# Conditioning rows on GpSimd's queue, eight weight sums shifted, the first head's weights written ahead of its tables, one Silu a gate chunk

## The chip, the cores and the metric

One core of one Trainium2 chip runs the kernel. The metric is device time of one execution in microseconds; three runs of the kernel before took 1923.67, 1926.17 and 1926.65 us, so the median is 1926.17 us. A further execution was taken with the hardware profiler, and all rows of a profile come from it. Its own time is 1929.21 us, and 1927.4 us of that are the span between its first and its last recorded instruction.

TensorE is called PE in the profile (PEld are its weight loads), VectorE is DVE, ScalarE is ACT, GpSimd is POOL and SyncE is SP. SP issues most of the loads from memory; ACT and POOL issue some transfers of their own.

## The reference

Two layers over 256 latent and 256 context tokens of width 2048. In each layer the tokens are normalised and modulated by a shift and a scale that come from a conditioning vector, then mixed, multiplied by a Silu gate, projected back, and added under a third conditioning vector, the output gate. Layer 0 mixes by retention in two directions (8 heads, keys of 256, values of 512), layer 1 by windowed attention (16 query heads, 4 key heads).

```
mod_l = silu(c) @ ada_w[i] + ada_b[i]         # shift, scale, gate of the latent tokens
mod_c = silu(c_ctx) @ ada_w[i] + ada_b[i]     # the same for the context tokens
h_l = rms_norm(x, g[i]) * (1 + sc_l) + sh_l
h_c = rms_norm(ctx, g[i]) * (1 + sc_c) + sh_c
layer 0: p = h @ ret_w_in                     # q, k, v, gate; 2048 x 12288
         o_c, s_f, s_b = retention(q_c, k_c, v_c)     # both directions
         o_l = retention(q_l, k_l, v_l, from s_f, s_b)
         y = (rms_norm(o) * silu(gate)) @ ret_w_out   # latent and context tokens
layer 1: o = attention(q, k, v within 128 tokens, all context keys, a sink)
         y = (o * silu(gate)) @ attn_w_out            # latent tokens alone
x = x + gt * y
```

Everything is fp32.

## The kernel before, in words

**Arithmetic.** Each fp32 operand of a matrix product is split into a high and a low part of a shorter type, and each product is three matmuls (`mm3`, L152 to L154: high by high, high by low, low by high). A weight arrives as a "piece" of 128 x 1024 numbers (512 KB): `load_raw` (L133 to L136) issues its load on SP into one of five buffers `wraw`; `split_w` makes the high part `wh` by a cast on ACT (L144) and the low part `wl` by a subtraction on DVE (L115), three buffers each. So a piece goes SP, DMA, ACT, DVE, PE.

**Stages**, with the times at which they run in the trace: the conditioning of layer 0 and the normalised tokens (to about 140 us), queries and keys of two heads (to about 240), the values (to about 548), the heads' gates, queries, keys and retention (to about 1165), the output projections of layer 0 (to about 1500), keys and values of layer 1, then its gates, queries and attention (about 1610 to 1845) and its output projection.

**The values** are computed for two heads at a time, four pairs, by a scheme that saves multiplications (Winograd's): weight pieces are added and subtracted on DVE into `vt` (L118), and these sums are split and multiplied. `VORDER` sets the order of the steps of a pair: four quarters, of 8, 8, 8 and 4 products X, Y, Z, each followed by `wide_hook`. A name such as "0X1" is quarter 0, product X, piece 1. Twelve matmuls make a step. Two tables say at which steps the hook also does other work: `WIDE_ADA` a step of the conditioning, `WIDE_SUMS` a weight sum.

**The conditioning of later parts** (`ada_parts`, L677 to L700) runs beside the values and the heads: pieces of `ada_w` are loaded by SP into the same `wraw` buffers, and DVE multiplies each by a conditioning row and adds up along it (L692). A row is 4 KB in memory, spread over all 128 partitions as it is loaded (`crow`, L672 to L675, 512 KB written); there is one for the latent and one for the context tokens, for each half of the width.

**Weight sums** (`sum_jobs`, L324 to L340) prepare weights for the output projections: a 256 KB half piece of the output weight is copied to memory by a transfer that ACT issues (L332), and three sums later POOL issues a transfer that adds a second half piece on top (L338). Ahead of each of these POOL makes a small copy (`pin`, L336) out of the newest `wl`, which keeps the transfer at its place. There are 128 sums. 14 are made beside each pair of values, others beside the heads, and what is left in the output projections' own stages.

**The heads** call `hook` (L1149) once per weight piece: up to hook 32 every second one makes a sum, from there on two of three (hooks count on to 88). The first head's gate is `gemm_ws(w0_d, 2, ...)`; ahead of it the program loads a table for the rotary embedding (`ropeR`, L953, L954) and the stored queries and keys (`qkr`, L1124).

**Layer 1's gates**: `gate(c)` (L1525 to L1531) makes four accumulators of 128 x 512; for each it copies the context half to `sgT` on ACT, adds the latent half on DVE, and applies Silu on ACT to a 128 x 256 tile. Between chunks ACT also computes the softmax's exponentials (L1563), which need another function table; ACT_TABLE_LOAD rows are the changes of table.

What the program's text says is not the final order: a scheduler puts each engine's instructions into a sequence by their dependences. The orders shown below are those sequences.

Of the kernel before, what the change touches and what calls it, by code (L numbers as in the profile page):

```python
# [14 lines left out]
AF = mybir.ActivationFunctionType  # L15
# [14 lines left out]
PUMP = 2  # L30
VORDER = ("X0 Z0 X1 Z1 X2 Z2 X3 Z3", "Y0 Z0 Y1 Z1 Y2 Z2 Z3 Y3", "X0 Y0 X1 Y1 X2 Y2 X3 Y3", "Y0 Y1 Y2 Y3")
WIDE_ADA = "3Y0 3Y1 3Y2 1Z0 1Z1 1Z2".split()
WIDE_SUMS = "0X1 0X3 1Y0 1Y1 1Z1 1Y2 1Z3 1Y3 2Y1 2Y2 2Y3 3Y1 3Y2 3Y3".split()
ASCALE = 128.0 ** -0.5


# [17 lines left out]
def backbone(ctx: ExitStack, tc, xT_d, w0_d, wo0_d, w1_d, wo1_d, adaS_d, adaB_d,  # L54
# [78 lines left out]
    def load_raw(src):  # L133
        t = strm.tile([P, 2, 512], F32, name="wraw", tag="wraw", bufs=5)
        nc.sync.dma_start(out=t, in_=src)
        return t  # L136

    def load_w(src):
        return split_w(load_raw(src))
# [13 lines left out]
        nc.tensor.matmul(ps, lhsT=ah, rhs=bl, start=False, stop=False, skip_group_check=skip)  # L153
        return nc.tensor.matmul(ps, lhsT=al, rhs=bh, start=False, stop=stop, skip_group_check=skip).ins  # L154

    def gemm_ws(w_d, chunk, nkp, moving, n, hook=None, pre=None, tail=1):


        accs = [acc_tile()[:, :n] for _ in range(4)]
        w = {}  # L160
        for kp in range(nkp):
            if pre is not None:
                pre(kp)
            w[kp] = load_w(w_d[chunk, kp])
            if kp < nkp - tail:
                kps = [kp]
            elif kp < nkp - 1:
                if hook is not None:
                    hook()
                continue  # L170
            else:
                kps = range(nkp - tail, nkp)
            for j in range(4):
                for kb in [2 * k + k2 for k in kps for k2 in range(2)]:
                    wh, wl = w[kb // 2]
                    js = slice(j * P, (j + 1) * P)
                    mm3(accs[j], (wh[:, kb % 2, js], wl[:, kb % 2, js]), moving(kb),
                        start=(kb == 0), stop=(kb == 2 * nkp - 1))
            if hook is not None:
                hook()  # L180
        return accs
# [215 lines left out]
    with tc.tile_pool(name="pa", bufs=1) as pa:  # L397
# [25 lines left out]
        def keep_warm(src, n=512):  # L423

            with after():
                pe[0] = nc.tensor.matmul(warm[:, :n], lhsT=ident, rhs=src[:, :n], start=True, stop=True).ins
# [146 lines left out]
        keep_warm(x01[:, 0, :])  # L573

        def first():
            keep_warm(x01[:, 1, :])
            strip(0, [2, 3])
            return pe[0]

# [87 lines left out]
    pb_cm.__exit__(None, None, None)  # L667


    rows_at = {}  # L670

    def crow(pool, tag, t, q, queue=nc.sync):  # L672
        c = pool.tile([P, 1024], F32, name="crow", tag=tag)
# [3 lines left out]
    def ada_parts(parts, ntk):  # L677
        for layer, kind in parts:
            part = 3 * layer + kind - 2
            asum = const.tile([P, 2, KB, ntk], F32, name="asum", tag=f"asum{ntk}")  # L680
            for q in range(2):
                if q not in rows_at:
                    rows_at.clear()
                    rows_at[q] = [crow(adap[0], f"crow{t}", t, q) for t in range(ntk)]
                    yield "row"
                for kb in range(KB):
                    raw = load_raw(adaB_d[16 * part + kb, q].rearrange("p (a c) -> p a c", a=2))
                    yield "load"
                    for t in range(ntk):
                        flat = raw.rearrange("p a c -> p (a c)")  # L690
                        junk = adap[0].tile([P, 1024], BF16, name="ajunk", tag="ajunk") if t < ntk - 1 else flat
                        nc.vector.scalar_tensor_tensor(  # L692
                            out=junk, in0=flat, scalar=1.0, in1=rows_at[q][t],
                            op0=ALU.mult, op1=ALU.mult, accum_out=asum[:, q, kb, t:t + 1])
                        if (kb, t) != (KB - 1, ntk - 1):
                            yield
                if q:
                    sh, gs, gt = (sh0, gs0, gt0) if layer == 0 else (sh1, gs1, gt1)
                    nc.vector.tensor_tensor(out=asum[:, 0], in0=asum[:, 0], in1=asum[:, 1], op=ALU.add)
                    ada_mod(kind, layer, 0, KB, asum[:, 0], sh, gs, gt, ntk)  # L700
                yield "end"
# [241 lines left out]
    def prep(m, us):  # L943
# [3 lines left out]
        for i, u in enumerate(us):  # L947
            b = unit(m, u)
            with behind():
                split(b[:, :, 0:L], b[:, :, L:T], raw[:, i])  # L950

    if True:
        ropeR = pb.tile([P, 2, 68], F32, name="ropeR")  # L953
        nc.sync.dma_start(out=ropeR, in_=ropeR_d)  # L954
# [193 lines left out]

        def hook():  # L1149
            state["n"] += 1  # L1150
            if state["n"] % 2 == 0 if state["n"] <= 32 else state["n"] % 3 < 2:
                next(sums, None)
            ada_step(next(state["ada"]))
            for x in next(state["plan"]):
                x()
# [12 lines left out]
        for h in range(H):  # L1168
# [12 lines left out]
            else:  # L1181
# [4 lines left out]
                if h == H - 1:  # L1186
                    break
                begin([[], [], [], [sc[0]], [sc[1]], [sc[2]], [sc[3]], []], (1, 3, 3, 2, 2, 2, 2, 3))
            accs = gemm_ws(w0_d, 3 * h + 2, 8, h_mov, T, hook=hook)
            sg = gates(h)  # L1190
            for j in range(4):
                nc.scalar.activation(sg[j // 2][:, j % 2, :], accs[j], AF.Silu)
# [273 lines left out]
    with tc.tile_pool(name="pe", bufs=1, side="right") as pe:  # L1466
# [58 lines left out]
        def gate(c):  # L1525
            accs = gemm_ws2(w1_d, 2 + c, 8, 0, hook=hook1)
            for j in range(4):
                z = sgT[:, 4 * c + j, :]
                nc.scalar.copy(z, accs[j][:, L:T])
                nc.vector.tensor_tensor(out=z, in0=accs[j][:, 0:L], in1=z, op=ALU.add)  # L1530
                nc.scalar.activation(z, z, AF.Silu)  # L1531

        def queries(c):
            accs = gemm_ts(w1_d, 6 + c, 8, h1_stat, 2, hook=hook1)
# [212 lines left out]
```

## Time and profile before

| what | value |
| --- | --- |
| runs | 1923.67, 1926.17, 1926.65 us; median 1926.17 us |
| profiled execution | 1929.21 us, its span 1927.4 us |
| PE busy | 1906.4 us, 99% of the span |
| PE's weight loads | 1577.9 us, 82% |
| DVE busy | 1477.2 us, 77% |
| ACT busy | 822.0 us, 43% |
| POOL busy | 324.5 us, 17% |
| mean granted clock of PE | 0.998 |
| bytes moved by DMA | 472.82 MB, mean 245 GB/s |

PE's row in the page's picture of 40 slices shows 8 tenths in the first slice and 9 or more in every other. The chain of waits, which follows the end of the span back to what released it, is 89% PE, 5% DMA and 3% DVE.

How to read the rows: a timeline row has the start in us, the duration, the engine, the line of the program, the operation, and out<-in with the shape; the square bracket holds the idle time before and what ended it. A window row has the stretch, its length, busy time and instruction count of each engine, then PE's granted clock (1.00 is full speed), the mean busy share of the 16 DMA engines, and GB/s. A row of the waits has total, count and longest in us. A row of the DMA issues has the KB of one and its us from issue to landing.

### The profile page before, as it was taken

What the parts mean: (1) busy time and instruction counts of PE and PEld (TensorE: products, weight loads), DVE (VectorE), ACT (ScalarE), POOL (GpSimd) and SP (SyncE); (2) the same over time, 40 slices, a digit from 0 to 9 for tenths busy, and PEclk for the clock granted to TensorE, in tenths of its full rate; (3) what the DMA queues carried; (4) which work ended last, traced back from release to release, by engine and by line L of the source; (5) the groups of instructions that cost most, each with busy time, mean ns of one, the idle gap of its engine ahead of it and who ended that gap; (6) DMA issues with size and microseconds to landing.
All of it is one profiled execution on the core that took longest, in us unless ns stands there. A gap on an engine that the chain in (4) does not pass through costs nothing.

```text
span 1927.4 us, 25993 instructions
## 1 busy us (share of the span) xinstructions
PE 1906.4 (99%) x9420; PEld 1577.9 (82%) x9420; DVE 1477.2 (77%) x2248; ACT 822.0 (43%) x1188; POOL 324.5 (17%) x418
## 2 busy tenths in 40 slices
PE   8999999999999999999999999999999999999999
PEld 4678887888878888888888888888888888888888
DVE  5568876877858888797978676877779668988764
ACT  4232333443434333232323244555545335666653
POOL 1201112222222233323232211000000100000000
PEclk9999999999999999999999999999999999999999
DMA  9968788899897777888888765789975356665454
GB/s 391 415 260 281 254 241 268 262 275 292 248 276 246 238 237 220 252 261 252 269 248 264 241 214 196 244 274 301 305 256 199 115 175 240 216 220 177 140 202 150
DMA packets 139217, 472.82 MB, mean 245 GB/s; under 512 B 17696, under 2 KB 32576, under 8 KB 133456
## 3 DMA queue, kind: packets, MB, share of 16 engines
q1 hardware_dynamic: 107104, 368.31, 54.2%
q0 software_dynamic: 15424, 49.33, 13.2%
q10 hardware_dynamic: 16560, 53.51, 8.0%
q8 instruction: 74, 1.21, 0.2%
q14 instruction: 55, 0.45, 0.1%
HBM read 440.09 MB, written 99.14 MB: 280 GB/s over the span
## 4 chain that ended last, share of the span: by engine, by line
PE 89%; DMA 5%; DVE 3%; issue 1%; ACT 1%; SPq 0%; DVEq 0%; ACTq 0%
PE acc L153 15%; PE acc L154 15%; PE acc L152 15%; PE acc L1253 9%; PE acc L205 6%; PE acc L1250 5%; PE pm L152 4%; PE pm L153 4%; PE pm L154 4%; DMA wraw<-in_w 3%; PE acc L202 3%; PE acc L534 2%; PE pm L1253 2%; DVE wl L115 1%; PE pm L471 1%; DMA araw<-in_adaS 1%
## 5 line engine op out<-in xcount | busy, mean ns | idle before, releaser
L144 ACT CAST wh<-wraw 128x1024 fp32r<-128x1024 f32 x415 | 434.8, 1052 | 678.0 <-DMA wraw<-in_w 185.4
L115 DVE TENSOR_TENSOR wl<-wraw,wh 128x1024 fp32r<-128x1024 f32 x416 | 509.8, 1229 | 234.8 <-ACT wh L144 230.8
L152 PE MATMUL acc<-hT_h,wh 128*128 128x512 f32 x928 | 363.7, 392 | 1.0 <-ACT wh L144 1.0
L154 PE MATMUL acc<-hT_h,wl 128*128 128x512 f32 x928 | 362.2, 390 | 0.6 <-DVE wl L115 0.6
L153 PE MATMUL acc<-hl,wh 128*128 128x512 f32 x928 | 361.9, 390 | 0.0
L336 POOL COPY pin_t<-wl 128x1 f32<-128x1 f32 x128 | 78.2, 611 | 758.0 <-DVE wl L115 748.1
L154 PEld LDWEIGHTS acc<-hT_h,wl 128*128 128x128 f32 x928 | 174.5, 188 | 38.1 <-DVE wl L115 1.3
L152 PEld LDWEIGHTS acc<-hT_h,wh 128*128 128x128 f32 x928 | 174.8, 188 | 37.6 <-ACT wh L144 1.5
L153 PEld LDWEIGHTS acc<-hl,wh 128*128 128x128 f32 x928 | 174.8, 188 | 34.9
L692 DVE SCALAR_TENSOR_TENSOR wraw<-wraw,crow 128x1024 f32<-128x1024 f32 x128 | 159.4, 1245 | 0.3
L692 DVE SCALAR_TENSOR_TENSOR ajunk<-wraw,crow 128x1024 bf16<-128x1024 f32 x96 | 124.5, 1297 | 4.1 <-DMA wraw<-in_adaB 3.9
L154 PE MATMUL acc<-wh,hl 128*128 128x512 f32 x320 | 125.7, 393 | 0.0
L338 POOL DMA_DIRECT2D wS_d<-in_wo x128 | 101.5, 794 | 20.8 <-issue 18.6
L255 POOL TENSOR_TENSOR rs<-ms,mhalf 128x4 f32<-128x4 f32 (+1 forms) x23 | 30.7, 1333 | 386.4 <-DVE ms L249 297.4
L144 ACT CAST wh<-vt 128x1024 fp32r<-128x1024 f32 x48 | 50.6, 1053 | 79.0 <-PE acc L154 30.5
L153 PE MATMUL acc<-wl,hT_h 128*128 128x512 f32 x192 | 76.6, 399 | 4.6 <-DVE wl L115 4.5
L152 PE MATMUL acc<-wh,hT_h 128*128 128x512 f32 x192 | 75.5, 393 | 0.6 <-ACT wh L144 0.6
L153 PE MATMUL acc<-wl,hl 128*128 128x512 f32 x192 | 75.1, 391 | 0.0
L152 PE MATMUL acc<-wh,hl 128*128 128x512 f32 x192 | 75.0, 391 | 0.0
L152 PE MATMUL pm<-r_h 128*128 128x512 f32 (+1 forms) x216 | 74.5, 345 | 0.0
L153 PE MATMUL pm<-r_l,r_h 128*128 128x512 f32 (+1 forms) x216 | 74.2, 343 | 0.1
L154 PE MATMUL pm<-r_h,r_l 128*128 128x512 f32 (+1 forms) x216 | 73.9, 342 | 0.0
(324 smaller groups left out, 3612.4 us busy)
## 6 DMA issues: line engine op xcount, KB each, us to landing
wraw<-in_w SPq DMA_DIRECT2D x288, 512.0 KB, 5.1
wraw<-in_adaB SPq DMA_DIRECT2D x128, 512.0 KB, 4.8
wraw<-in_wo SPq DMA_DIRECT2D x80, 512.0 KB, 4.5
wS_d<-in_wo ACTq DMA_DIRECT2D x128, 256.0 KB, 4.9
wS_d<-in_wo POOLq DMA_DIRECT2D x128, 256.0 KB, 6.5
wraw<-wS_d SPq DMA_DIRECT2D x64, 512.0 KB, 5.3
araw<-in_adaS SPq DMA_DIRECT2D x28, 1024.0 KB, 13.1
wraw<-uB_d SPq DMA_DIRECT2D x20, 512.0 KB, 4.7
```

What stands on the lines that cost most here:

```text
L115: return nc.vector.tensor_tensor(out=out, in0=a, in1=hi.bitcast(F32), op=ALU.subtract)
L144: last_hi[0] = nc.scalar.copy(wh, raw).ins
L152: nc.tensor.matmul(ps, lhsT=ah, rhs=bh, start=start, stop=False, skip_group_check=skip)
L153: nc.tensor.matmul(ps, lhsT=ah, rhs=bl, start=False, stop=False, skip_group_check=skip)
L154: return nc.tensor.matmul(ps, lhsT=al, rhs=bh, start=False, stop=stop, skip_group_check=skip).ins
L202: nc.tensor.matmul(accs[j][:, 0:L], lhsT=wk, rhs=h1(kb, s)[:, 0], start=False, stop=(kb == 2 * nkp - 1))
L205: nc.tensor.matmul(accs[j], lhsT=wk, rhs=h1(kb, s).rearrange("p a t -> p (a t)"), start=(kb == 0), stop=False)
L336: pin = nc.gpsimd.tensor_copy(pin_t, last_wl[0][:, 0, 0:1].bitcast(F32)).ins
L338: nc.gpsimd.dma_start(out=wS_d[i, r, q, x], in_=wo0_d[(*SUMS[i][1], r, q, x)], accum_op=ALU.add, max_dma_last_dim=4096)
L692: nc.vector.scalar_tensor_tensor(out=junk, in0=flat, scalar=1.0, in1=rows_at[q][t], op0=ALU.mult, op1=ALU.mult, accum_out=asum[:, q, kb, t ...
L1250: last_pe[0] = nc.tensor.matmul(accs[j][:, 0:L], lhsT=wk, rhs=b[:, 0:L], start=False, stop=(kq == 3 and k == 3)).ins
L1253: nc.tensor.matmul(accs[j], lhsT=wk, rhs=b, start=(kq == 0 and k == 0), stop=False)
```

## The change

Five edits:

1. `WIDE_SUMS` loses "0X1" and "0X3", so each pair of values makes 12 sums instead of 14. In the heads, from hook 33 on, four of five hooks make a sum instead of two of three. 117 sums instead of 118 are issued by the end of the heads.
2. The first three gate pieces of the first head are loaded by a line ahead of the table `ropeR`, and `gemm_ws` takes them over (`raws`).
3. The first two conditioning rows that `ada_parts` loads stay on SP; all later ones are issued by GpSimd.
4. One of the matmuls that only warm PE at the start is gone (`keep_warm(x01[:, 1, :])`).
5. `gate(c)` applies one Silu to the 128 x 1024 of a chunk instead of four to 128 x 256 each.

```
-WIDE_SUMS = "0X1 0X3 1Y0 1Y1 1Z1 1Y2 1Z3 1Y3 2Y1 2Y2 2Y3 3Y1 3Y2 3Y3".split()
+WIDE_SUMS = "1Y0 1Y1 1Z1 1Y2 1Z3 1Y3 2Y1 2Y2 2Y3 3Y1 3Y2 3Y3".split()
...
-    def gemm_ws(w_d, chunk, nkp, moving, n, hook=None, pre=None, tail=1):
+    def gemm_ws(w_d, chunk, nkp, moving, n, hook=None, pre=None, tail=1, raws=()):
...
-            w[kp] = load_w(w_d[chunk, kp])
+            w[kp] = split_w(raws[kp]) if kp < len(raws) else load_w(w_d[chunk, kp])
...
         def first():
-            keep_warm(x01[:, 1, :])
             strip(0, [2, 3])
...
-    rows_at = {}
+    rows_at, queue = {}, [nc.sync]
...
-                    rows_at[q] = [crow(adap[0], f"crow{t}", t, q) for t in range(ntk)]
+                    rows_at[q] = [crow(adap[0], f"crow{t}", t, q, queue[0]) for t in range(ntk)]
+                    queue[0] = nc.gpsimd
...
+    early = [load_raw(w0_d[2, kp]) for kp in range(3)]
     if True:
         ropeR = pb.tile([P, 2, 68], F32, name="ropeR")
...
-            if state["n"] % 2 == 0 if state["n"] <= 32 else state["n"] % 3 < 2:
+            if state["n"] % 2 == 0 if state["n"] <= 32 else state["n"] % 5 < 4:
...
-            accs = gemm_ws(w0_d, 3 * h + 2, 8, h_mov, T, hook=hook)
+            accs = gemm_ws(w0_d, 3 * h + 2, 8, h_mov, T, hook=hook, raws=early if h == 0 else ())
...
-                nc.scalar.activation(z, z, AF.Silu)
+            z = sgT[:, 4 * c:4 * c + 4, :]
+            nc.scalar.activation(z, z, AF.Silu)
```

**The order on SP and POOL at the start of the second pair of values.** `wraw<-in_w0` are weight pieces of layer 0, `wraw<-in_adaB` pieces of the conditioning's weight, `crow<-crow_d` conditioning rows. SP before:

```order
L135 DMA wraw_2487<-in_adaB 128x1024
L135 DMA wraw_2492<-in_w0 128x1024
L135 DMA wraw_2515<-in_w0 128x1024
L135 DMA wraw_2540<-in_w0 128x1024
L674 DMA crow_2785<-crow_d_108 128x1024
L135 DMA wraw_2561<-in_w0 128x1024
L135 DMA wraw_2583<-in_w0 128x1024
L135 DMA wraw_2604<-in_w0 128x1024
```

SP now:

```order
L135 DMA wraw_2480<-in_adaB 128x1024
L135 DMA wraw_2485<-in_w0 128x1024
L135 DMA wraw_2508<-in_w0 128x1024
L135 DMA wraw_2533<-in_w0 128x1024
L135 DMA wraw_2554<-in_w0 128x1024
L135 DMA wraw_2576<-in_w0 128x1024
L135 DMA wraw_2594<-in_w0 128x1024
```

POOL now, where each `pin_t` and `wS_d` belong to a weight sum:

```order
L336 COPY pin_t_98<-wl_2488 128x1
L338 DMA wS_d_101<-in_wo0 64x1024
L673 DMA crow_2772<-crow_d_108 128x1024
L336 COPY pin_t_98<-wl_2513 128x1
L338 DMA wS_d_101<-in_wo0 64x1024
L336 COPY pin_t_98<-wl_2695 128x1
L338 DMA wS_d_101<-in_wo0 64x1024
L673 DMA crow_2774<-crow_d_108 128x1024
```

The row is gone from SP and stands on POOL between two sums; the second one, for the context tokens, follows it there two sums later. In all, four rows leave SP: these two, and two of layer 1's conditioning.

**SP where the heads begin.** `wraw<-in_w0` are now the first head's gate pieces, `wraw<-v_d` stored values, `ropeR` the table, `qkr` the stored queries and keys. Before:

```order
L135 DMA wraw_4325<-in_w0 128x1024
L135 DMA wraw_4355<-in_w0 128x1024
L135 DMA wraw_4388<-in_w0 128x1024
L135 DMA wraw_4429<-in_w0 128x1024
L135 DMA wraw_4475<-v_d_103 128x1024
L135 DMA wraw_4477<-v_d_103 128x1024
L954 DMA ropeR_4310<-in_ropeR 128x136
L1124 DMA qkr_4317<-qk_d_104 128x2x512
L1124 DMA qkr_4319<-qk_d_104 128x2x512
L135 DMA wraw_4479<-in_w0 128x1024
```

Now:

```order
L135 DMA wraw_4285<-in_w0 128x1024
L135 DMA wraw_4287<-in_w0 128x1024
L135 DMA wraw_4289<-in_w0 128x1024
L135 DMA wraw_4404<-in_w0 128x1024
L135 DMA wraw_4450<-v_d_103 128x1024
L135 DMA wraw_4452<-v_d_103 128x1024
L955 DMA ropeR_4291<-in_ropeR 128x136
L1125 DMA qkr_4298<-qk_d_104 128x2x512
L1125 DMA qkr_4300<-qk_d_104 128x2x512
L135 DMA wraw_4454<-in_w0 128x1024
```

The kinds of loads stand in the same sequence; the first three pieces have other buffer numbers.

**ACT at the third gate chunk of layer 1.** `sgT` is the gate, `prob` the softmax, `r2z_h` the high part of something that PE transposes next. Before:

```order
L1529 COPY sgT<-acc 128x256 x2
L1531 ACT_TABLE_LOAD
L1531 ACTIVATE sgT<-sgT 128x256
L1563 ACT_TABLE_LOAD
L1563 ACTIVATE prob,sm<-pm,nm 128x512
L1570 ACTIVATE es<-es 128x4
L1531 ACT_TABLE_LOAD
L1531 ACTIVATE sgT<-sgT 128x256
L1578 ACTIVATE prob<-prob,es 128x512 x2
L1529 COPY sgT<-acc 128x256 x2
L121 CAST r2z_h<-pm 128x512 x2
L1531 ACTIVATE sgT<-sgT 128x256 x2
```

Now:

```order
L1530 COPY sgT<-acc 128x256 x2
L1565 ACTIVATE prob,sm<-pm,nm 128x512
L1572 ACTIVATE es<-es 128x4
L1530 COPY sgT<-acc 128x256 x2
L144 CAST wh<-wraw 128x1024
L1580 ACTIVATE prob<-prob,es 128x512 x2
L1533 ACT_TABLE_LOAD
L1533 ACTIVATE sgT<-sgT 128x1024
L121 CAST r2z_h<-pm 128x512 x3
```

Two changes of table are gone; the Silu stands behind the softmax and directly ahead of the casts.

## The prediction

> **What bounds the kernel now.** I read the page's head first, then its chain of waits, then the table of 50 us windows, and only then the narrow windows, timelines and waits of the places that the diff touches.
>
> ```profile
> span 1927.4 us, 25993 instructions
> ...
> PE 1906.4 (99%) x9420; PEld 1577.9 (82%) x9420; DVE 1477.2 (77%) x2248; ACT 822.0 (43%) x1188; POOL 324.5 (17%) x418
> ...
> PE 89%; DMA 5%; DVE 3%; issue 1%; ACT 1%; SPq 0%; DVEq 0%; ACTq 0%
> ```
>
> PE is busy for 1906.4 of 1927.4 us. The change takes no matmul of weight away, so it can win only out of the 21.0 us in which PE stands idle, and out of matmuls that run slowly because the granted clock falls after a stall. The windows (us, then PE busy with its matmuls, PEld, DVE, ACT, POOL, granted clock, DMA share, GB/s) say where that lies.
>
> ```profile
> 0.00:50.00 50.00, 40.62 (x226) 21.36 (x230) 26.56 (x66) 20.39 (x30) 5.97 (x11) 1.00 0.98 392
> ...
> 300.00:350.00 50.00, 46.08 (x195) 37.30 (x194) 34.83 (x36) 18.02 (x19) 8.94 (x17) 0.97 0.86 259
> ...
> 550.00:600.00 50.00, 48.39 (x211) 39.45 (x210) 30.51 (x48) 16.87 (x23) 7.51 (x14) 0.97 0.85 270
> ...
> 1750.00:1800.00 50.00, 49.14 (x248) 40.69 (x247) 40.35 (x77) 36.78 (x62) 1.18 (x2) 1.00 0.50 171
> ```
>
> Idle of PE: 9.4 us in the first 50, 3.9 around the start of the second pair of value heads, 1.6 where the heads begin, 0.9 at layer 1's gates. These four are the places of the diff. Only 300 to 350 and 550 to 600 also show a clock under 1.00.
>
> **Edit A: the conditioning rows leave SP.** The second pair starts near 310. The same columns, in 4 us windows:
>
> ```profile
> 316.00:320.00 4.00, 4.00 (x19) 3.30 (x19) 0.72 (x1) 0.00 (x0) 0.96 (x2) 1.00 1.04 390
> 320.00:324.00 4.00, 2.39 (x10) 1.42 (x8) 0.10 (x1) 1.04 (x1) 0.00 (x0) 1.00 0.96 319
> 324.00:328.00 4.00, 1.69 (x6) 1.38 (x7) 3.95 (x4) 2.00 (x2) 0.00 (x0) 0.89 0.60 221
> 328.00:332.00 4.00, 4.00 (x14) 3.18 (x13) 3.09 (x4) 1.05 (x1) 0.00 (x0) 0.68 0.77 246
> 332.00:336.00 4.00, 4.00 (x20) 3.30 (x19) 2.48 (x3) 1.64 (x2) 0.96 (x2) 1.00 0.71 217
> ```
>
> The first and last rows give 39 matmuls in 8 us, 0.205 us each. The 12 us between hold 10 + 6 + 14 = 30 matmuls where 12 / 0.205 = 58.5 would fit: 28.5 x 0.205 = 5.85 us are lost, of which 3.9 are idle and 1.9 come from the clock of 0.89 and 0.68. What ends the longer wait, and what fed it (timeline of PE and DVE, then SP's queue; the bracket is the idle time before and its releaser):
>
> ```profile
> 326.31 0.51 PE L153 MATMUL acc<-wl,hT_h 128*128 128x512 f32 x1 [3.33 <-DVE wl L115]
> ...
> 323.89 1.22 DVE L118 TENSOR_TENSOR vt<-wraw 128x1024 f32<-128x1024 f32 x1 [7.18 <-DMA wraw<-in_w]
> ...
> 302.30 0.33 SPq L135 DMA_DIRECT2D wraw<-in_w  x1
> 306.43 0.33 SPq L674 DMA_DIRECT2D crow<-crow_d  x1
> 307.57 1.46 SPq L135 DMA_DIRECT2D wraw<-in_w  x2
> ```
>
> PE waits for a split, the split for VectorE's sum of two weight pieces, and that for a weight load 7.18 us. The late loads stand on SP just behind the conditioning row. Their landing times (narrow views of the DMA issues: KB each, us from issue to landing), the crow's, those of the two loads behind it, and of loads in the third pair's start, where no row is loaded:
>
> ```profile
> crow<-crow_d SPq DMA_DIRECT2D x1, 512.0 KB, 11.6
> wraw<-in_w SPq DMA_DIRECT2D x1, 512.0 KB, 13.7
> wraw<-in_w SPq DMA_DIRECT2D x1, 512.0 KB, 15.1
> ...
> wraw<-in_w SPq DMA_DIRECT2D x2, 512.0 KB, 11.2
> ```
>
> So the row landed at 306.43 + 11.6 = 318.0, 3.8 us behind the load ahead of it (302.30, landed at about 314.2), and the two loads behind it at 321.3 and 323.8. Without the row in that line they come up to 3.8 us earlier, at 317.5 and 320.0, and the 3.33 us wait at 323 to 326 has its cause gone. SP's own wait for the row's buffer frees nothing, since the next load would have waited as long:
>
> ```profile
> SPq L674 <- DVE ajunk L692: 3.7, 1, 3.7
> ```
>
> What is late next: starts of pairs that have no row in the way still lose a little (PE's columns only).
>
> ```profile
> 404.00:408.00 4.00, 3.32 (x15) 1.00 0.78 224
> 480.00:484.00 4.00, 3.74 (x17) 1.00 0.94 282
> ```
>
> They lose (19.5 - 15) x 0.205 = 0.9 and (19.5 - 17) x 0.205 = 0.5 us. I expect the second pair to look like them: 5.85 less about 0.45 leaves **5.4 us**; the bounds are 0 (the row only moves to another queue of the same DMA engines) and 5.85. The row itself is not urgent, on whichever queue; VectorE first multiplies by it here:
>
> ```profile
> 383.69 1.21 DVE L692 SCALAR_TENSOR_TENSOR ajunk<-wraw,crow 128x1024 bf16<-128x1024 f32 x1
> ```
>
> GpSimd issues it between two weight sums. Behind it wait only pin copies and accumulations, whose results nobody reads before the output projections.
>
> The Trainium skill bears on this from both sides. "DMA: Bandwidth & Descriptors", section "Issuing engines are not separate DMA queues", says that transfers of all engines run on the same 16 DMA engines and that another issuer mostly saves issue time: by it, A would be worth 0.33 us, the row's issue on SP. The section "Queues, rings and completion order" of the same page says that a DMA engine takes turns between the queues it has work for, one packet each: by it, a load behind the row no longer waits for the whole row, but shares with it. The trace shows a DMA share of 0.96 to 1.04 before and in the stall, which speaks for the first, and only 0.60 to 0.77 behind it.
>
> **Edit B: no weight sums at X1 and X3 of a pair's first quarter.** Two sums less in each pair's first 8 steps, eight in all. In the second pair their two transfers each (an ACT-issued copy and a GpSimd-issued accumulation) fall into the stall of A already counted; in the third and fourth they lie around the 0.9 and 0.5 us above. I take **1.0 us** of these 1.4 (bounds 0 and 1.4).
>
> Seven of the eight go to the heads, where four hooks of five now issue a sum, and one into the output projections. The queues of the accumulations and of the copies took this share of 16 engines' span:
>
> ```profile
> q0 software_dynamic: 15424, 49.33, 13.2%
> ...
> q10 hardware_dynamic: 16560, 53.51, 8.0%
> ```
>
> At most 21.2% of 1927 us for 128 sums is 3.2 us a sum; seven more, over 330 us of heads, are 0.07 of DMA share on top of this:
>
> ```profile
> 800.00:1130.00 330.00, 330.00 (x1530) 275.57 (x1529) 263.79 (x447) 103.20 (x163) 93.30 (x111) 1.00 0.82 252
> ```
>
> PE does not idle there for a moment. The smallest margin that I found between a weight's split and the matmul that uses it:
>
> ```profile
> 1025.30 1.22 DVE L115 TENSOR_TENSOR wl<-wraw,wh 128x1024 fp32r<-128x1024 f32 x1
> ...
> 1029.12 0.39 PE L154 MATMUL acc<-hT_h,wl 128*128 128x512 f32 x1
> ```
>
> It is 1029.12 - 1026.52 = 2.6 us, more than a load lengthens by if a share of 0.82 becomes 0.89. So **0**; the bound on the loss is a rival below.
>
> **Edit C: the first head's gate pieces ahead of its tables.** The stall where the heads begin (PE's columns, then SP's issues):
>
> ```profile
> 570.00:575.00 5.00, 3.39 (x9) 0.79 0.94 288
> 575.00:580.00 5.00, 5.00 (x21) 0.87 0.91 292
> ...
> 559.34 0.33 SPq L954 DMA_DIRECT2D ropeR<-in_ropeR  x1
> 561.08 1.06 SPq L135 DMA_DIRECT2D wraw<-in_w  x2
> ```
>
> 30 matmuls where 10 / 0.205 = 48.8 fit: 3.85 us lost, fed by the two pieces issued at 561.08 behind table and value loads. But the order of SP, shown above, has four gate pieces ahead of the table before the change already, and the same sequence after it: four pieces, two value loads, the table, two q/k loads, then the next pieces. Nothing moves, so **0**, with 3.85 as the upper bound.
>
> **Edit D: one Silu a gate chunk.** ScalarE's groups (busy and mean ns), then the one stall at these gates:
>
> ```profile
> L1531 ACT ACT_TABLE_LOAD x5 | 6.4, 1283 | 0.1
> L1531 ACT ACTIVATE sgT<-sgT 128x256 f32<-128x256 f32 x16 | 6.3, 422 | 0.1
> ...
> 1764.00:1768.00 4.00, 3.14 (x21) 1.00 0.00 0
> ...
> 1767.95 0.66 PE L1583 MATMUL pm<-ident,prob 128*128 128x128 f32 x4 [0.86 <-DVE r2z_l L115]
> ```
>
> Sixteen activations of 0.42 us become four longer ones, and two table loads of 1.28 us go. ScalarE has room almost everywhere (36.8 of 50 us busy in this very window), so only the 0.86 us count. At the third gate chunk the table loads that stood ahead of the softmax are gone, but the whole Silu now stands ahead of the casts r2z_h, which feed that same wait through VectorE: at worst a load and the work of four pieces, 1.28 + 4 x 0.42 = 3.0 us, is put in front. The matmuls that wait are also placed earlier in PE's order. I take **0.4 us** (bounds -3.0 and 0.86).
>
> **Edit E: one warming matmul less at the start.** In the first 50 us the DMA share is 0.98: PE waits for weights, not for its own work. A warming matmul takes half of this row:
>
> ```profile
> 18.96 1.10 PE L426 MATMUL pm<-x,ident 128*128 128x512 f32 x2
> ```
>
> So **0**, with its own 0.55 us as the bound on either side: gained, or lost again if the clock is granted that much later.
>
> **The sum.** 5.4 + 1.0 + 0 + 0.4 + 0 = 6.8 us. The profiled execution took 1929.21 us (1.8 more than its span); less 6.8 this is 1922.4, with a span of 1920.6. It was 3.0 us above the median of the runs, 1926.17, so the median should come out at 1926.17 - 6.8 = 1919.4. What a measurement of this kernel can tell from no change is about 0.2%, 3.85 us: faster means under 1922.3, slower over 1930.0.
>
> **The rivals.**
>
> *The row's bytes compete all the same (0.20).* The DMA engines are full until 324 in any queue, the two loads behind the row land as late as now, and A is worth nothing. For it: the share of 0.96 to 1.04. Against it: the row holds back its successors by 3.8 us on their own queue, and two sums leave the same stretch. B and D remain: 1926.17 - 1.4 = 1924.8, no change that can be told.
>
> *The early pieces do take effect (0.06).* If the first pieces are issued sooner in time, though not in another order, the 3.85 us of C come on top: 1919.4 - 3.85 = 1915.6. Against it: the unchanged order.
>
> *The heads pay for the sums (0.08).* With four hooks in five a GpSimd accumulation and a copy stand beside nearly each weight load of the later heads. If a load comes more than the 2.6 us of margin late, PE stalls and its clock falls as it does at 570, 3.85 us each time; once in each of heads 4 to 7 it is 15.4 - 6.8 = 8.6 us more than now, 1934.8. It decides from a loss of 6.8 + 3.85 = 10.65 us, three such stalls. For it: VectorE is 80% busy there and the DMA share grows. Against: not one idle moment of PE in 330 us today.
>
> **How the numbers follow.** The forecast has 0.66, with its own range of 1917 to 1923: A between 3 and 5.85, B and D near their values. Of its 0.66 about 0.56 lie under 1922.3. With the 0.06 of the early pieces, faster has 0.62. Slower has the heads' 0.08, and no change the rest, 0.30. The range must leave no more than 0.2 out: it reaches up to 1925.5, past the first rival, and down to 1916, just short of the second.
>
> **What would show it.** A: no row of SP loads a crow after the first two; in the 12 us of the second pair's start some 56 matmuls at a clock of 1.00, the loads landing in 10 to 12 us instead of 13.7 and 15.1. B: the windows that answer to 404 and 480 full; heads without an idle moment at a share near 0.88. C: the same 30 matmuls in 10 us. D: ten table loads instead of twelve, the 0.86 us wait gone or shorter. The prediction is wrong if the second pair still stalls for 3 us, if PE idles in the heads, or if the time lies above 1925.5.

## The result

The changed kernel took 1923.82 us (median of 21 runs, 1919.86 to 1931.93), the kernel before 1928.54 us (21 runs, 1923.67 to 1936.44). The ratio is 0.9975, with a 95% interval of 0.9966 to 0.9985: 0.25% faster, 4.8 us of 1928.5, with bounds of 2.9 and 6.6 us. Forecast were 6.8 us (1919.4 from 1926.17) and a range of 1916.0 to 1925.5. Run again for the experiments, the same kernel gave 0.9976 (0.9965 to 0.9986).

The profiled execution of the changed kernel took 1922.0 us. That is 7.2 us less than the profiled one of before, more than the medians differ: before's lies 0.7 us above its median, this one 1.8 us below. Head and chain of the page of the changed kernel:

```profile
span 1920.1 us, 25990 instructions
...
PE 1902.3 (99%) x9418; PEld 1576.4 (82%) x9418; DVE 1477.6 (77%) x2248; ACT 817.4 (43%) x1174; POOL 326.7 (17%) x422
...
PE 94%; DMA 3%; DVE 2%; issue 1%; ACT 0%; SPq 0%; POOL 0%; DVEq 0%; ACTq 0%
```

PE idles for 17.8 us instead of 21.0, and its busy time is 4.1 us shorter: two warming matmuls are gone, and PE ran at half clock for one stretch of 3.4 us instead of two. The 50 us windows that answer to those shown of before:

```profile
0.00:50.00 50.00, 40.02 (x212) 22.10 (x216) 26.64 (x66) 20.47 (x30) 5.97 (x11) 0.97 0.98 390
...
300.00:350.00 50.00, 49.54 (x218) 40.49 (x217) 38.01 (x38) 19.93 (x20) 9.54 (x16) 1.00 0.87 267
...
550.00:600.00 50.00, 48.77 (x219) 39.59 (x217) 34.05 (x59) 19.13 (x29) 6.50 (x12) 1.00 0.85 259
...
1750.00:1800.00 50.00, 50.00 (x267) 42.65 (x265) 40.17 (x71) 34.40 (x56) 2.02 (x2) 1.00 0.52 179
```

The window from 300 to 350 has 49.5 us of PE instead of 46.1, and 218 matmuls instead of 195. The one at layer 1's gates has no idle time left. The clock of 0.97 in the first window is that one stretch, near 24 us; the first profile of before had none there. The second pair's start in 4 us windows:

```profile
316.00:320.00 4.00, 4.00 (x20) 3.30 (x19) 1.03 (x1) 1.05 (x1) 0.00 (x0) 1.00 1.03 348
320.00:324.00 4.00, 3.54 (x16) 2.63 (x15) 3.25 (x3) 1.97 (x2) 0.00 (x0) 1.00 0.80 301
324.00:328.00 4.00, 4.00 (x19) 3.30 (x18) 4.00 (x5) 1.08 (x2) 0.00 (x0) 1.00 0.83 261
328.00:332.00 4.00, 4.00 (x19) 3.31 (x18) 3.07 (x3) 2.24 (x4) 0.00 (x0) 1.00 0.51 190
332.00:336.00 4.00, 4.00 (x20) 3.30 (x19) 3.34 (x5) 1.99 (x2) 0.91 (x2) 1.00 0.30 79
```

Between 320 and 332 stand 16 + 19 + 19 = 54 matmuls at a clock of 1.00, where there had been 30. The wait that remains (PE's timeline), and the loads that feed it (the row, now on GpSimd's queue, and the two weight loads that used to stand behind it):

```profile
323.11 0.50 PE L153 MATMUL acc<-wl,hT_h 128*128 128x512 f32 x1 [0.46 <-DVE wl L115]
...
crow<-crow_d POOLq DMA_DIRECT2D x1, 512.0 KB, 11.1
wraw<-in_w SPq DMA_DIRECT2D x1, 512.0 KB, 8.6
wraw<-in_w SPq DMA_DIRECT2D x1, 512.0 KB, 11.4
```

3.33 us have become 0.46; the loads land in 8.6 and 11.4 us instead of 13.7 and 15.1.

Where the heads begin, three stretches of the windows (all engines), then PE's waits:

```profile
564.00:569.00 5.00, 3.78 (x15) 2.48 (x15) 3.44 (x5) 3.85 (x5) 0.00 (x0) 1.00 0.93 284
569.00:574.00 5.00, 5.00 (x23) 4.13 (x22) 4.62 (x9) 0.62 (x1) 0.97 (x2) 1.00 0.97 293
598.00:602.00 4.00, 2.72 (x13) 2.01 (x12) 3.86 (x9) 2.77 (x5) 1.94 (x3) 1.00 0.74 253
...
PE pm L152 <- ACT r_h L121: 1.2, 1, 1.2
PE acc L152 <- ACT wh L144: 0.6, 1, 0.6
PE acc L154 <- DVE wl L115: 0.6, 1, 0.6
```

The first stall is 1.2 us instead of 1.6 and did not take the clock down, but a wait of 1.2 us for `r_h` stands near 600, where the kernel before had next to none.

To see where the time went I matched the matmuls of two profiles one by one and took the lead in us that the later one has at the same matmul. The lead of the changed kernel over the one before, by stage: start (to 60 us) -1.1; to the second pair +0.5; the second pair's start (318 to 345) **+5.3**; the third pair's start (400 to 420) +1.0; the fourth pair -1.1, and +0.7 behind it; where the heads begin (556 to 640) +2.0, then -1.5; heads and output projections -0.2; layer 1's gates (1740 to 1800) **+1.5**. With smaller pieces between (0.1 and 0.2) the sum is 7.6. The same table is made below for each experiment.

### The profile page after: what moved, and what is told of

It is laid out like the page before. It is cut to its first block, busy times and chain, and to the rows that moved or that the text cites. A ratio compares the mean times of both kernels' runs of the same rounds, so it can differ in the third digit from the quotient of the medians.

```text
span 1920.1 us, 25990 instructions
## 1 busy us (share of the span) xinstructions
PE 1902.3 (99%) x9418; PEld 1576.4 (82%) x9418; DVE 1477.6 (77%) x2248; ACT 817.4 (43%) x1174; POOL 326.7 (17%) x422
## 4 chain that ended last, share of the span: by engine, by line
PE 94%; DMA 3%; DVE 2%; issue 1%; ACT 0%; SPq 0%; POOL 0%; DVEq 0%; ACTq 0%
PE acc L153 16%; PE acc L152 16%; PE acc L154 16%; PE acc L1254 9%; PE acc L205 6%; PE acc L1251 5%; PE pm L152 5%; PE pm L153 5%; PE pm L154 5%; PE acc L202 3%; PE acc L534 2%; DMA wraw<-in_w 2%; PE pm L1254 2%; PE pm L471 1%; PE pm L1251 1%; PE pm L1585 1%
```

## The experiments

Each ran beside the kernel before on the same chip; a ratio is to that one. Two theories stood at first. Mine: the conditioning row holds back the loads behind it in SP's queue, and taking it out gives 5.4 us; the sums matter for the third and fourth pair only. The rival: the bytes of row and sums fill the DMA engines, on whichever queue, and what helps is that sums leave the place.

**The kernel before, again**, with no edit.

> The kernel before, once more, so that a second profile of it tells what belongs to the program and what to one execution. Every theory: ratio 1.000 within 0.001. If the stall at the second pair's start (5.85 us lost) belongs to the program it comes again within 0.5 us; the same for the 3.85 us lost where the heads begin. If one of them differs by more than 1 us, a difference of that size between before and the change at that place says nothing of the change.

Measured: ratio 1.000 (0.9989 to 1.0011). The second pair's stall came again, 3.35 us of wait and a clock of 0.50 behind it. The heads' start did not: this execution leads the first by 1.6 us there, without any edit. So what one profile shows between 556 and 640 says nothing of the change, nor do the 1.1 us at the start, which this one lost as well (1.2; its clock in the first 50 us is 0.97 too).

**The row alone on GpSimd's queue.**

```
-    rows_at = {}
+    rows_at, queue = {}, [nc.sync]
...
-  ... crow(adap[0], f"crow{t}", t, q) ...
+  ... crow(adap[0], f"crow{t}", t, q, queue[0]) ...
+                    queue[0] = nc.gpsimd
```

> The kernel before with edit 3 alone (the conditioning rows after the first two on GpSimd's queue). My theory (the row in SP's queue holds back the two weight loads behind it): the stall at the second pair's start shrinks from 5.85 us to under 1.5, although the two weight sums are still made there, and the time falls by 4 to 6 us, ratio 0.997 to 0.998. Rival (the bytes of row and sums fill the DMA engines, whatever queue they are on, and it was the sums that left): the stall stays above 3 us and the ratio is 0.999 to 1.000.

Measured: ratio 0.9987 (0.9977 to 0.9996). The stall stayed. From the profile of this kernel: the row's landing, those of the two loads, PE's wait, what VectorE did ahead of it, and PE's columns behind it:

```profile
crow<-crow_d POOLq DMA_DIRECT2D x1, 512.0 KB, 13.3
wraw<-in_w SPq DMA_DIRECT2D x1, 512.0 KB, 10.1
wraw<-in_w SPq DMA_DIRECT2D x1, 512.0 KB, 13.7
...
326.76 0.79 PE L153 MATMUL acc<-wl,hT_h 128*128 128x512 f32 x1 [2.76 <-DVE wl L115]
...
324.35 1.23 DVE L118 TENSOR_TENSOR vt<-wraw 128x1024 f32<-128x1024 f32 x1 [5.67 <-DMA wraw<-in_w]
325.49 1.22 DVE L115 TENSOR_TENSOR wl<-wraw,wh 128x1024 fp32r<-128x1024 f32 x1
...
326.00:329.00 3.00, 2.24 (x5) 0.52 0.88 291
329.00:332.00 3.00, 3.00 (x8) 0.50 0.72 212
```

The first load gains 3.6 us (13.7 to 10.1), as I had said of both; the second, which is the one that PE waits for, gains 1.4 (15.1 to 13.7). What PE waits for is the low part `wl` of the first load's piece. That load had landed at 319.55, but VectorE's sequence has the sum `vt`, which needs both pieces, ahead of this split (324.35, then 325.49): so it is by VectorE's order that the second load decides. No run changed that order.

PE idles here for 2.76 us instead of 3.9, yet its lead over this place is only 0.2 us, because in this execution the clock stayed at 0.50 for 6.8 us behind the wait, and in the first profile of before for 3.4. My theory of one cause falls: it names a true effect, with a third of its size for the load that counts. Of the 2.5 us of the ratio (0.8 to 4.4) this profile shows 1.0 us at the third pair's start, and the rest at no place that can be told from the scatter of single profiles.

**The changed kernel with the row back on SP**, that is the other four edits.

```
-                    queue[0] = nc.gpsimd
```

> The changed kernel with edit 3 undone (all those rows on SP again), everything else as changed. My theory: the stall at the second pair's start comes back with 4.5 to 6 us, though the sums 0X1 and 0X3 are gone, and the time lies within 0.15% of the kernel before. Rival (the sums made the stall): the stall stays away, ratio 0.997 to 0.998.

**Edit 1 alone**, the sums.

```
-WIDE_SUMS = "0X1 0X3 1Y0 1Y1 ...
+WIDE_SUMS = "1Y0 1Y1 ...
...
-  ... if state["n"] <= 32 else state["n"] % 3 < 2:
+  ... if state["n"] <= 32 else state["n"] % 5 < 4:
```

> The kernel before with edit 1 alone (two weight sums less beside each pair, four hooks of five in the heads). My theory: the second pair's stall stays at 5 us or more; the losses at the starts of the third and fourth pair (0.9 and 0.5 us) shrink by about 0.6 together; no PE idle time in heads 1 to 7; ratio 0.999 to 1.000. Rival (sums made the second pair's stall): it shrinks under 2 us, ratio 0.997 to 0.998. Second rival (the heads pay for the sums): idle time of PE between 650 and 1150 us, ratio above 1.001.

Measured: ratios 0.9990 (0.9980 to 1.0001) with the row back and 0.9998 (0.9985 to 1.0010) with the sums alone. In both the stall shrank without the row having moved. With edit 1 alone, the two loads, PE's wait, and a window in the later heads:

```profile
wraw<-in_w SPq DMA_DIRECT2D x1, 512.0 KB, 12.8
wraw<-in_w SPq DMA_DIRECT2D x1, 512.0 KB, 12.9
...
324.84 0.50 PE L153 MATMUL acc<-wl,hT_h 128*128 128x512 f32 x1 [2.05 <-DVE wl L115]
...
850.00:900.00 50.00, 49.23 (x234) 1.00 0.94 281
```

The load that counts gains 2.2 us (15.1 to 12.9 in both kernels); the wait is 2.05 us (2.04 in the other kernel) and PE's lead there 2.1 and 2.2 us. Neither theory holds alone: row and sums are two parts of one overload. Over all profiles that load took 14.2 to 15.1 us with neither edit (three profiles), 13.7 with the row moved (one), 12.9 without the two sums (two), and 11.4 to 13.0, 12.1 on average, with both (eight). The second thing to see is new: PE idles in heads 4 to 7, where it did in neither profile of before. The second rival of that run was right in its idle time, not in its ratio: between 640 and 1150 the sums alone lost 2.6 us and the other kernel 1.4, and the sums alone are worth nothing that the ratio shows.

**One Silu a gate chunk, alone.**

```
-                nc.scalar.activation(z, z, AF.Silu)
+            z = sgT[:, 4 * c:4 * c + 4, :]
+            nc.scalar.activation(z, z, AF.Silu)
```

> The kernel before with edit 5 alone (one Silu a gate chunk). In the two profiles with this edit PE gained 1.5 us between 1740 and 1800 us of the kernel before, in the three without it 0.0. Theory (it is the Silu): again 1.5 us there, the wait of 0.86 us gone, nothing elsewhere, ratio 0.999 to 0.9995. Rival (another edit moves PE's order there): less than 0.4 us.

Measured: ratio 0.9991 (0.9981 to 1.0001), and 1.5 us of lead between 1740 and 1800. Each of the ten profiles with this edit gains 1.5 there, and the three without it 0.0 or 0.1.

**The extra sums in the first stage of the output projections** instead of the heads.

```
-  ... if state["n"] <= 32 else state["n"] % 5 < 4:
+  ... if state["n"] <= 32 else state["n"] % 3 < 2:
...
-                    if len(ms) == 1 and kq == 2:
+                    if kq == 2 or len(ms) == 2 and kq == 0:
```

> The changed kernel with the eight sums not in the heads (two of three hooks again) but in the first stage of the output projections, where the DMA share is 0.57 to 0.71 (two sums in each quarter of it). Theory (the heads pay a little for the denser sums, 1.4 and 2.6 us in two profiles, 0 in that of the change): no PE idle time between 850 and 1000 us, and a time 0 to 2 us under the changed kernel's, ratio to before 0.9965 to 0.9975. Rival (those waits in the heads were chance): the same time as the changed kernel, 0.9975. Second rival (the output projections pay instead): PE idle between 1165 and 1250, ratio above 0.998.

Measured: ratio 0.9992 (0.9981 to 1.0002). No idle time in the heads, but this in the first stage of the output projections (PE's columns, then PE's waits):

```profile
1150.00:1200.00 50.00, 49.27 (x258) 1.00 0.62 204
1200.00:1250.00 50.00, 47.76 (x272) 1.00 0.86 269
1250.00:1300.00 50.00, 48.41 (x279) 1.00 0.92 290
...
PE pm L1254 <- DVE x L1260: 3.8, 2, 2.2
```

PE loses 5.7 us there. A free share of the DMA engines was no sign of room: PE waits there until VectorE has emptied an accumulator that it needs again (L1260), and in VectorE's sequence that stands behind a difference of two weight pieces (L118). In one of the two waits that difference had itself waited 1.7 us for a weight load.

**The table and the first q/k loads on GpSimd's queue**, so that SP does not wait for the values' store ahead of the next gate pieces.

```
-        nc.sync.dma_start(out=ropeR, in_=ropeR_d)
+        nc.gpsimd.dma_start(out=ropeR, in_=ropeR_d)
...
-                nc.sync.dma_start(out=qkr[h, i], ...
+                (nc.sync if h else nc.gpsimd).dma_start(out=qkr[h, i], ...
```

> The changed kernel with the table ropeR and the first head's two q/k loads on GpSimd's queue, so that the next two gate pieces stand directly behind the value loads on SP. In the order of the kernel before they were issued at 561.08, behind a wait of SP for the store of values, 7.9 us. Theory (that wait feeds the stall where the heads begin): the pieces are issued some 6 us sooner, the waits of 1.03 and 0.58 us go; but VectorE has no free time from 575 to 605, so most of it comes back as a wait near 600, and the whole gain is 0.5 to 1 us. Rival (the gain stays): 2 to 3.85 us, ratio to before 0.9955 to 0.9965. Second rival (the first q/k loads come later and the first head's scores wait): no gain or a loss.

**Both of the last two.**

> The two last edits together on the changed kernel. Theory: their effects add, 0.5 to 3 us under the changed kernel, ratio to before 0.996 to 0.997. Rival: neither does anything that can be measured, 0.9975.

Measured: ratios 0.9969 (0.9959 to 0.9979) and 0.9988 (0.9978 to 0.9999). The pieces were issued from 548.02 on, 6.7 us sooner than at 554.72 in the changed kernel. SP in the first of these two, and where PE waits between 545 and 640:

```profile
544.60 2.06 SPq L135 DMA_DIRECT2D wraw<-v_d  x2
548.02 4.19 SPq L135 DMA_DIRECT2D wraw<-in_w  x2
...
PE pm L152 <- ACT r_h L121: 0.5, 1, 0.5
PE acc L154 <- DVE wl L115: 0.3, 1, 0.3
```

0.8 us of waits instead of 2.4. But in the profiles of the other kernel with this edit they are 3.1 us, and the ratio of the first is not to be told from the changed kernel's. In the same profile the later heads lost 5.9 us, the most of all:

```profile
850.00:900.00 50.00, 48.82 (x233) 1.00 0.92 271
900.00:950.00 50.00, 49.29 (x222) 1.00 0.81 257
```

The second kernel joins the loss of the output projections (4.0 us) to the rest, and is slower than the first.

**The changed kernel, again.**

> The changed kernel once more, for a second profile of it and beside the three others. Profiles with four hooks of five so far lost 0, 1.4, 2.6 and 5.8 us of PE in heads 4 to 7, those with two of three 0, 0, 0, 0, 0 and 1.4. Theory (the denser sums make these heads marginal, so that an execution loses there by chance): again a loss of 0 to 6 us there, and the pair's start and the gates as in the first profile (5.3 and 1.5 us gained); ratio 0.997 to 0.998.

Measured: ratio 0.9976 (0.9965 to 0.9986). Its second pair's start is not that of the first profile. The row, the two loads, PE's wait, and PE's columns behind it:

```profile
crow<-crow_d POOLq DMA_DIRECT2D x1, 512.0 KB, 12.4
wraw<-in_w SPq DMA_DIRECT2D x1, 512.0 KB, 10.1
wraw<-in_w SPq DMA_DIRECT2D x1, 512.0 KB, 13.0
...
325.57 0.72 PE L153 MATMUL acc<-wl,hT_h 128*128 128x512 f32 x1 [2.07 <-DVE wl L115]
...
326.00:329.00 3.00, 3.00 (x8) 0.50 0.91 289
```

The same program, but the second load took 13.0 us, the wait was 2.07 us, and the clock behind it fell to a half. PE's lead is 2.1 us instead of 5.3.

**The two sums left out of the second pair alone** (28 steps make a pair), `WIDE_SUMS` and the heads as before.

```
-            if f"{g}{m}{kp}" in WIDE_SUMS:
+            if f"{g}{m}{kp}" in WIDE_SUMS and not ((n - 1) // 28 == 1 and g == 0 and m == "X"):
...
-  ... if state["n"] <= 32 else state["n"] % 5 < 4:
+  ... if state["n"] <= 32 else state["n"] % 3 < 2:
```

> The changed kernel, but the sums X1 and X3 left out in the second pair alone, where the conditioning row is loaded; the other three pairs make 14 sums as before and the heads two of three hooks, so that two sums more fall to the output projections. Theory (only the second pair's two sums and the row had to go, and the denser sums of the heads cost about 2 us on average): second pair's start as in the changed kernel, at most 1 us lost at the third and fourth, no loss in heads 4 to 7; 1 to 2 us under the changed kernel, ratio 0.996 to 0.997. Rival (the sums at the other pairs' starts cost more than the heads): the same as the changed kernel or slower, 0.9975 to 0.999.

**The same, with the table and q/k loads on GpSimd.**

> The kernel of e13 with the table ropeR and the first head's q/k loads on GpSimd's queue as in e11. Theory (what is won where the heads begin comes back near 600, since VectorE is full there): within 0.1% of e13. Rival (it stays): 1 to 2 us under e13.

**The extra sums in heads 0 to 3.**

```
-  if state["n"] % 2 == 0 if state["n"] <= 32 else state["n"] % 5 < 4:
+  if state["n"] % (2 if state["n"] <= 8 else 4) != 1 if state["n"] <= 32 else state["n"] % 3 < 2:
```

> The changed kernel with its extra sums in heads 0 to 3 (22 sums in their 32 hooks instead of 16), where the DMA share is 0.72 to 0.79, and two of three hooks in heads 4 to 7. Theory (heads 4 to 7 have too little margin, heads 0 to 3 have more): no loss in the profile between 850 and 1000, 1 to 2 us under the changed kernel, ratio 0.996 to 0.997. Rival (VectorE, full where the heads begin, is held up by the later loads): a wait of PE over 1 us more between 570 and 780, no gain over the changed kernel.

Measured: 0.9975 (0.9966 to 0.9984), 0.9975 (0.9965 to 0.9985) and 0.9971 (0.9960 to 0.9982), medians of 1923.12, 1923.84 and 1922.95 us beside 1922.32 for the changed kernel. None beats it by more than the intervals hold. All three have heads without a loss. The first two lose 2.4 and 1.9 us at the fourth pair (the changed kernel 1.1 and 0.6, the kernel before, again, 1.1); the third gives nothing back that I can see, but no gain can be told either: by its ratio it is 0.05% ahead of the changed kernel beside it, by its median 0.6 us behind. The e14 edit moved the wait where the heads begin, as said, but neither way by more than the profiles of one kernel differ.

**All profiles side by side.** Lead over the first profile of the kernel before, in us, worked out as above; the wait and the time at a granted clock of 0.50 are those of the second pair's start.

| kernel | longest wait | us at a clock of 0.50 | 2nd pair 318 to 345 | 3rd pair 400 to 420 | 4th pair 420 to 500 | heads begin 556 to 640 | heads 640 to 1150 | gates 1740 to 1800 |
| --- | --- | --- | --- | --- | --- | --- | --- | --- |
| before, first | 3.33 | 3.4 | 0 | 0 | 0 | 0 | 0 | 0 |
| before, again | 3.35 | 6.8 | -0.6 | -0.2 | -1.1 | 1.6 | 0.0 | 0.1 |
| Silu alone | 3.27 | 3.4 | 1.2 | 0.2 | -0.8 | 0.9 | 0.0 | 1.5 |
| row alone | 2.76 | 6.8 | 0.2 | 1.0 | 0.5 | 2.3 | 0.0 | 0.0 |
| sums alone | 2.05 | 3.4 | 2.1 | 1.0 | -1.6 | 1.8 | -2.6 | 0.0 |
| change, row back | 2.04 | 3.4 | 2.2 | 1.0 | -1.3 | 1.1 | -1.4 | 1.5 |
| change, first | 0.46 | 0 | 5.3 | 1.0 | -1.1 | 0.5 | 0.0 | 1.5 |
| change, again | 2.07 | 3.4 | 2.1 | 1.0 | -0.6 | 0.3 | -0.2 | 1.5 |
| sums in projections | 0.91 | 0 | 4.9 | 0.9 | 0.5 | 2.4 | 0.0 | 1.5 |
| table on GpSimd | 0.67 | 0 | 5.1 | 1.0 | 0.6 | 2.7 | -5.9 | 1.5 |
| both of these | 0.59 | 0 | 5.2 | 0.9 | -0.7 | 0.2 | -1.4 | 1.5 |
| second pair's sums only | 1.79 | 3.4 | 2.4 | 1.0 | -2.4 | 1.5 | 0.0 | 1.5 |
| the same, table on GpSimd | 1.56 | 0 | 4.3 | 0.9 | -1.9 | 0.4 | 0.0 | 1.5 |
| sums in heads 0 to 3 | 1.31 | 0 | 4.5 | 0.6 | -0.8 | 0.0 | 0.0 | 1.5 |

With the row moved and the second pair's sums gone (the last eight rows) the second pair's start gains 4.2 us on average; the three without either have 0.2: 4.0 us for the two edits. The changed kernel's own two profiles have 5.3 and 2.1. The third pair's start gains 0.9, by either edit. The five profiles with four hooks of five in the heads lose 2.0 us between 640 and 1150 on average (0, 0.2, 1.4, 2.6, 5.9), the nine others 0.2 (eight of them 0, and 1.4 in one): 1.9 us, from few and scattered numbers. The gates give 1.5. Sum: 4.0 + 0.9 - 1.9 + 1.5 = 4.5 us, beside 4.8 measured. That this comes so near is partly luck: the two profiles of the changed kernel itself lost only 0 and 0.2 us in the heads, and without the 1.9 the sum is 6.4, which the interval of 2.9 to 6.6 allows as well.

## Why the prediction was right or wrong

The direction, the forecast of faster and the range hold; 6.8 us were a little more than the 2.9 to 6.6 that the interval leaves. The time of 1919.4 us was 4.4 us too low, and 2.4 of these are not the change's: three runs had put the kernel before at 1926.17 us, 21 runs put it at 1928.54. By the prediction's own line for faster, 1922.3, the 1923.82 us taken alone would be no change; it is the runs of both kernels side by side that tell the difference. And the range says little for A, since it reached past the first rival (1924.8), in which A is worth nothing.

**A (forecast 5.4, bounds 0 and 5.85).** The edits of A and B together give 4.0 at this place on average, but not by the step that I named. "Without the row in that line they come up to 3.8 us earlier" was true of the first load (3.6) and not of the second (1.4), on which the wait hangs. The 3.8 were misread besides: the load ahead of the row, issued at 302.30, landed 10.7 us later, at 313.0 and not at 314.2, so the row came 5.0 us behind it. And the 0.9 and 0.5 us lost at the other pairs have a mean of 0.7, where the sum took 0.45. Alone, A shortens PE's idle time by some 1.2 us; its one profile leads by 0.2. The first rival, the row's bytes compete all the same, had been nearer for this edit: the row alone on GpSimd's queue takes 13.3 us instead of 11.6 and shares with the loads. That rival, and the rule of the Trainium skill beside it ("DMA: Bandwidth & Descriptors", section "Issuing engines are not separate DMA queues"), say that only issue time is saved; the first load's 3.6 us and the second's 1.4 do not agree with that. The sharing by turns that the Trainium skill has on the same page ("DMA: Bandwidth & Descriptors"), section "Queues, rings and completion order", fits: the load next in line gains most, and the row pays for it.

**B (forecast 1.0 at the third and fourth pair, 0 in the second, 0 in the heads).** This is the step that failed. In the second pair I wrote that the two sums "fall into the stall of A already counted"; without them the load that counts came 2.2 us sooner, as against 1.4 without the row. The heads, which I put at 0, are not settled. The changed kernel's own two profiles lose 0 and 0.2 us there, as forecast; three kernels that issue the same sums in the heads lose 1.4, 2.6 and 5.9. So the reason given, a margin of 2.6 us at the smallest, is too weak: it came from one execution with fewer sums. The 1.9 us of the average would be the third rival's mechanism at an eighth of its price (15.4 us); but the kernels that took the denser sums out of the later heads were not measurably faster, so the runs do not show that the changed kernel pays it. Third and fourth pair: 0.9 and nothing, 1.0 had been taken, and the 0.9 come with the row alone as well.

**C (0).** No effect that shows. The sign given, the same 30 matmuls in 10 us, did not come (15 + 23 = 38 in the first profile), but edit 2 was not run alone, and the place scatters too much to say more: profiles with it gain 1.0 us between 556 and 640 on average (nine), those without it 1.3 (five).

**D (0.4, bounds -3.0 and 0.86).** 1.5 us in every profile: mis-sized, and over its upper bound, which counted the wait alone. The group of matmuls that waited was also placed elsewhere in PE's order, and that is most of the other 0.6 us. Before, the 16 transposes of `prob` stood in one run (its start is the first row below) that held PE for 3.05 us with the wait, from 1765.50 to 1768.55. Now they stand in four groups between products (the second row is the first group); each holds PE for 0.35 us and makes the next product 0.09 us longer, 1.8 us in all. The two groups on ScalarE are as expected, four table loads at the gates instead of five:

```profile
1765.50 1.59 PE L1583 MATMUL pm<-ident,prob 128*128 128x128 f32 x12
...
1756.26 0.60 PE L1585 MATMUL pm<-ident,prob 128*128 128x128 f32 x4
...
L1533 ACT ACT_TABLE_LOAD x4 | 5.1, 1283 | 0.1
L1533 ACT ACTIVATE sgT<-sgT 128x1024 f32<-128x1024 f32 x4 | 4.2, 1061 | 0.0
```

**E (0).** To 60 us the nine profiles without that call lose 1.1 us on average against the first profile of before, the other four that kept it 1.3: no effect. The call is two rows in the trace and 1.10 us, all of the row that the prediction took half of; the bound should have been twice as wide. Edit 4 was not run alone either.

So the sum was too high by what the second pair misses (1.4) and by whatever the heads lose (0.1 in the changed kernel's own profiles, 1.9 on the average of five), and too low by the gates (1.1). Errors of both signs are in it, and that the total came near is in part luck.

**What stays open.** Why moving the row alone gains 1.0 us at the third pair's start, where no row is loaded. Whether the loss in the later heads comes from the sums' bytes or from the order on VectorE; the waits seen were for `wl` and for `sg`, 1.1 us at most, in different places in each execution. And whether the second pair's wait would go if VectorE split the first piece ahead of the sum of both.

## What to carry to other kernels

When several transfers crowd in ahead of a deadline, find the one load that the bounding engine waits for and follow its own landing time: an edit that speeds up its neighbour by 3.6 us may speed it up by 1.4. Look also at the order of the engine in between: here the work on a piece that had long landed stood behind work that needed the next one. Two edits that each shorten a stall can be worth little one by one and much together, because a stall that stays long also costs clock (here 1.79 us did, 1.56 did not); so test them together as well as alone. A margin read from one execution is a sample: work that is moved into a stage "with no idle moment" needs a margin that holds in the worst execution of several.

## What was not expected of the hardware

At the second pair's start PE's clock behaves like a switch. In the eight profiles whose wait was 1.79 us or longer it fell to 0.50 and stayed there for 3.4 us, in two of them (before again, and the row alone) for 6.8; in the other six, with waits of 0.46 to 1.56 us, it never fell. The 0.89 and 0.68 of the prediction are windows that hold a part of one such stretch, 327.13 to 330.54. This row is from the kernel with a wait of 1.56 us (PE's columns):

```profile
326.00:329.00 3.00, 3.00 (x15) 1.00 0.79 253
```

and this one from that with 1.79 us:

```profile
326.00:329.00 3.00, 3.00 (x8) 0.50 0.84 262
```

The difference, 7 matmuls of 0.205 us = 1.4 us in that window alone, is why gains at this place come as about 2 or over 4 us, with little between, and why two edits that look additive in the load are not so in the time (0.2, 2.1, and 4.0 together). The idle time plus half of PE's busy time at 0.50 gives what a profile loses here: 3.9 + 1.7 = 5.6 us in the first of before, 2.8 + 3.1 = 5.8 with the row alone, 2.1 + 1.7 = 3.8 in the second of the changed kernel, 0.5 in its first; for all 14 the differences agree with the table to 0.4 us. The length of the wait does not decide alone: where the heads begin, two waits of 1.6 and 0.6 us left the clock at 1.00 in one profile (second pair's sums only) and took it to 0.50 in another (sums in heads 0 to 3). The Trainium skill, "TensorE: Matmul & The Clock Gate", Part 1, has the clock halve after about 3.4 us of idle time in a window that runs free of the kernel: the halving and the part that chance plays agree, but 1.79 us of waiting were enough here.

A profile of the same program differs from the next by up to 3 us at one stall (5.3 and 2.1 us of lead at the second pair) and by 1.6 us where the heads begin; over the later heads, kernels with the same sums there differ by 6 us. That is as much as the whole effect; only the medians of a dozen runs and more, and the same stage read in many profiles, told the edits apart.
